# Projection products handed out six matmuls at a time in a fused four-stage kernel

## The chip, the cores and the metric

The kernel runs on one core of a Trainium2 chip. The metric is the device time of one execution in microseconds; lower is better. PE is the matrix engine (TensorE), DVE, ACT and POOL are the vector, scalar and GpSimd engines, SP is the queue that issues most transfers.

## The reference, cut to what matters

Two transformer blocks of width 1024 over a sequence of 512. In the first, a projection of the input feeds an RWKV-7 mixer (8 heads of 64) and a block-sparse attention (MoBA, 4 heads of 128), whose outputs together go through an output projection; then an MLP, a dilated attention of 8 heads with its own projections, and an MLP again. In the second block one projection feeds four mixers (S5, HGRN, FoX and mLSTM), followed by an output projection and a gated MLP. The RWKV mixer is the part that matters most below; each of its heads runs this recurrence over the 512 positions:

```python
def step(S, inp):
    r_t, w_t, k_t, v_t, a_t, b_t = inp
    sa = jnp.einsum('bhvk,bhk->bhv', S, a_t)
    S = S * w_t[:, :, None, :] + sa[..., None] * b_t[:, :, None, :] + v_t[..., None] * k_t[:, :, None, :]
    return S, jnp.einsum('bhvk,bhk->bhv', S, r_t)
...
_, y = lax.scan(step, jnp.zeros((B, H, N, N), f32), xs)
...
y = ((y - mu) * lax.rsqrt(var + RWKV_GN_EPS)).reshape(B, T, RWKV_DIM) * lnx_g + lnx_b
...
return y * g
```

The second block's mixers end in `mix = jnp.concatenate([y_a, y_b, y_c, y_d], axis=-1) @ w_out[l]`, where `y_d` is a headwise normalised mLSTM output times a sigmoid gate.

## The kernel before

**Stages.** By the trace's clock: RWKV and MoBA with their projection 0 to 388 us, MLP to 800, dilated attention with its projection to 1129, MLP to 1529, the four mixers of the second block with their projection ("block 2") to 1833, output projection and gated MLP to 2228. All data is fp32; every large product is made of three matmuls on values split into a high and a low part (`wh`/`wl` for weights, `acth`/`actl` for activations). ACT writes the high part (L228, L238), DVE the low part (L230, L239).

**Projections as filler.** `Kern.stream` (L254 to 283) is a Python generator. A task is one projection tile of 128 output columns over all 512 positions: eight row tiles k of the contraction, three matmuls of 128x512 each (L272, L273, L274, PSUM tile `gemm`). After every row tile it yields 0.64, its own estimate of the microseconds just issued. At k = 0 it also issues the previous task's evacuation and the next weights' transfer, at k = 6 the next weights' split. `Kern.early` (L285 to 303) does the same for the first half of the columns of the output projection, over the row tiles of the mixers' output that are already there (tile `pjps`, L356 to 358); it yields 0.64 after three matmuls too, and `Kern.project` does the second half of the columns afterwards.

**The planner.** `Kern.race` (L305 to 347) decides in which order code is emitted. Its chains are generators for the mixers; a chain yields the PE time and the latency of the step just issued. A chain is taken when its operands should be there by the planner's clock; otherwise, or when the debt `owed` is over 0.6, one turn of the filler is taken:

```python
if self.gemm is not None and (i is None or ready[i] > t or owed > 0.6):
    r = next(self.gemm, None)
    ...
    if r:
        t, owed, stuck = t + r, owed - r, 0
        owed = max(owed, 0)
...
    if r[0]:
        t = at + r[0]
        owed += keep * r[0]
```

`keep` is 0.65 in the RWKV stage and 0.5 in the dilated stage and block 2. When `stream` is at its end, `over()` puts `early` in its place, and what chains are left after both go out with no filler. A scheduler then simulates the program and sets the final order on each engine from this order. PE runs its instructions strictly in that order.

**The RWKV chain.** Four pairs of heads go one after another through `core` (L571 to 739): the inverse of a triangular matrix in five levels (L604 to 632: product `pinv` L610, mask `pm` on DVE L614, product `pinv` L624, addition `yc` on DVE L628; the last level has half the products), then `pg` (L647), `ptu` (L658), `pmc` (L675 to 677), `pqt` (L693), a chain of states with `pst` (L714) and `py` (L703, L704) beside it, and `py` again (L732). `tail` (L741 to 780) normalises: a sum (L749), a square, a second sum, an inverse root in small DVE steps, a product (L764), transposes `pyt` (L768), the gate `pgt` (L773, L775), the last product `ymix` (L778) and its split (L238, L239), from which the output projection's products read. Only the last pair has no later pair's work behind it.

**The end of block 2.** After the mLSTM's last products `mlo` (L1666) come DVE and ACT steps (L1668 to 1678), a head norm (L1523 to 1536, last step L1535), transposes `bkp` (L1543) for two row tiles of the mixers' output, gain and gate (L1686, L1688) and the split.

Of the kernel before, what the change touches and what calls it, by code (L numbers as in the profile page):

```python
# [105 lines left out]
class Kern:  # L106
# [147 lines left out]
    def stream(self, win, tasks, x, first=None, late=None):  # L254


        nc = self.nc
        xh, xl = x
        w = first or self.wload(win, tasks[0][0])
        for i, task in enumerate(tasks):  # L260
            m, evac = task[1:3]
            if len(task) > 3 and not task[3]():
                if late and i:
                    late[0](late[1])
                    late = None
                while not task[3]():
                    yield 0
            nxt = None
            ps = self.psG.tile([P, 512], F32, name="gemm", tag="g")
            n = len(w)  # L270
            for k, (h, l) in enumerate(w):
                nc.tensor.matmul(ps[0:m], lhsT=h[:, 0:m], rhs=xh[:, k, :], start=k == 0, stop=False)  # L272
                nc.tensor.matmul(ps[0:m], lhsT=h[:, 0:m], rhs=xl[:, k, :], start=False, stop=False)  # L273
                nc.tensor.matmul(ps[0:m], lhsT=l[:, 0:m], rhs=xh[:, k, :], start=False, stop=k == n - 1)  # L274
                if k == 0 and late:
                    late[0](late[1])
                if k == 0 and i + 1 < len(tasks):
                    nxt = self.wfetch(win, tasks[i + 1][0])
                if k == n - 2 and nxt:
                    w = self.wsplit(nxt)  # L280
                yield 0.64
            late = (evac, ps)
        late[0](late[1])

# [2099 lines left out]
```

## Time and profile before

| | us |
|---|---|
| median of three runs (lowest, highest) | 2234.99 (2234.35, 2239.33) |
| the profiled execution | 2230.15 |
| its span on the core | 2228.0 |
| PE busy in it | 2160.5 |
| DVE, ACT, POOL busy | 1265.1, 758.6, 382.0 |

The times from the rows below belong to the profiled execution; the comparison with another kernel goes by the medians, which here lie 5 us higher. A busy share says little by itself: matmuls that overlap count once in "busy", and a PE that is busy at a lower granted clock ("PEclk", 1.00 is 2.4 GHz, 0.50 is 1.2 GHz) gets less done.

### The profile page before, as it was taken

What the parts mean: (1) busy time and instruction counts of PE and PEld (TensorE: products, weight loads), DVE (VectorE), ACT (ScalarE), POOL (GpSimd) and SP (SyncE); (2) the same over time, 40 slices, a digit from 0 to 9 for tenths busy, and PEclk for the clock granted to TensorE, in tenths of its full rate; (3) what the DMA queues carried; (4) which work ended last, traced back from release to release, by engine and by line L of the source; (5) the groups of instructions that cost most, each with busy time, mean ns of one, the idle gap of its engine ahead of it and who ended that gap; (6) DMA issues with size and microseconds to landing.
All of it is one profiled execution on the core that took longest, in us unless ns stands there. A gap on an engine that the chain in (4) does not pass through costs nothing.

```text
span 2228.0 us, 37413 instructions
## 1 busy us (share of the span) xinstructions
PE 2160.5 (97%) x15646; PEld 1709.3 (77%) x15646; DVE 1265.1 (57%) x2528; ACT 758.6 (34%) x1218; POOL 382.0 (17%) x399
## 2 busy tenths in 40 slices
PE   8999999999999999999999999998999998999997
PEld 6666667888878877777788888877667778888886
DVE  6576666764444765656574444466755566344445
ACT  4332333423322433333342233235434354222221
POOL 0011111370056242332130000011320021000001
PEclk9999999999999999999999999998899999999999
DMA  4111114342333322222243233213211232233321
GB/s 142 49 40 40 49 40 170 97 131 95 100 100 113 126 77 67 67 68 66 86 139 94 90 104 95 93 45 132 63 45 46 92 104 95 95 97 98 99 76 38
DMA packets 56088, 192.80 MB, mean 87 GB/s; under 512 B 8208, under 2 KB 8720, under 8 KB 55408
## 3 DMA queue, kind: packets, MB, share of 16 engines
q1 hardware_dynamic: 52384, 184.11, 25.6%
q0 software_dynamic: 3536, 6.32, 0.9%
q8 instruction: 122, 2.00, 0.4%
q14 instruction: 46, 0.38, 0.1%
HBM read 181.98 MB, written 8.39 MB: 85 GB/s over the span
## 4 chain that ended last, share of the span: by engine, by line
PE 79%; DVE 10%; issue 4%; ACT 3%; DMA 2%; POOL 2%; SPq 0%; DVEq 0%; ACTq 0%; POOLq 0%
PE gemm L272 6%; PE mlpo L356 6%; PE mlpo L357 6%; PE mlpo L358 6%; PE gemm L273 5%; PE gemm L274 5%; PE mlps L249 4%; PE mlps L250 4%; PE mlps L251 4%; PE ffg L250 2%; PE ffg L251 2%; PE ffg L249 2%; PE ffu L250 2%; PE ffu L251 2%; PE ffu L249 2%
## 5 line engine op out<-in xcount | busy, mean ns | idle before, releaser
L228 ACT CAST wh<-wr 128x1024 fp32r<-128x1024 f32 (+1 forms) x311 | 323.4, 1044 | 762.3 <-PE mlpo L358 247.5
L230 DVE TENSOR_TENSOR wl<-wr,wh 128x1024 fp32r<-128x1024 f32 (+1 forms) x285 | 354.9, 1246 | 359.9 <-ACT wh L228 270.2
L272 PE MATMUL gemm<-acth,wh 128*128 128x512 f32 (+1 forms) x672 | 306.1, 456 | 7.8 <-ACT acth L238 6.4
L274 PE MATMUL gemm<-acth,wl 128*128 128x512 f32 (+1 forms) x672 | 271.8, 404 | 4.5 <-DVE wl L230 4.5
L273 PE MATMUL gemm<-actl,wh 128*128 128x512 f32 (+1 forms) x672 | 272.4, 405 | 0.0
L356 PE MATMUL mlpo<-wh,mlph 128*128 128x512 f32 x688 | 270.2, 393 | 0.3 <-DVE xres L1039 0.3
L357 PE MATMUL mlpo<-wl,mlph 128*128 128x512 f32 x688 | 269.6, 392 | 0.0
L358 PE MATMUL mlpo<-wh,mlpl 128*128 128x512 f32 x688 | 269.4, 392 | 0.0
L249 PE MATMUL mlps<-acth,wh 128*128 128x512 f32 x448 | 176.3, 394 | 0.0
L251 PE MATMUL mlps<-acth,wl 128*128 128x512 f32 x448 | 176.2, 393 | 0.0
L250 PE MATMUL mlps<-actl,wh 128*128 128x512 f32 x448 | 176.1, 393 | 0.0
L272 PEld LDWEIGHTS gemm<-acth,wh 128*128 128x128 f32 (+1 forms) x672 | 128.9, 192 | 59.1 <-issue 24.7
L274 PEld LDWEIGHTS gemm<-acth,wl 128*128 128x128 f32 (+1 forms) x672 | 128.9, 192 | 36.0 <-DVE wl L230 5.8
L356 PEld LDWEIGHTS mlpo<-wh,mlph 128*128 128x128 f32 x688 | 129.4, 188 | 29.3 <-DVE xres L1039 0.4
L358 PEld LDWEIGHTS mlpo<-wh,mlpl 128*128 128x128 f32 x688 | 129.1, 188 | 29.1 <-DVE mlpl L239 0.2
L357 PEld LDWEIGHTS mlpo<-wl,mlph 128*128 128x128 f32 x688 | 129.2, 188 | 28.6
L230 POOL TENSOR_TENSOR wl<-wr,wh 128x1024 fp32r<-128x1024 f32 (+1 forms) x26 | 71.2, 2763 | 446.0 <-ACT wh L228 424.1
L273 PEld LDWEIGHTS gemm<-actl,wh 128*128 128x128 f32 (+1 forms) x672 | 129.9, 193 | 22.9 <-issue 4.4
L1039 DVE SCALAR_TENSOR_TENSOR xres<-xres,mlpo 128x512 f32<-128x512 f32 x120 | 82.1, 685 | 105.3 <-PE mlpo L358 104.3
L251 PEld LDWEIGHTS mlps<-acth,wl 128*128 128x128 f32 x448 | 84.1, 188 | 19.7
L250 PEld LDWEIGHTS mlps<-actl,wh 128*128 128x128 f32 x448 | 84.2, 188 | 19.4
L249 PEld LDWEIGHTS mlps<-acth,wh 128*128 128x128 f32 x448 | 84.1, 188 | 19.5
(617 smaller groups left out, 3901.9 us busy)
## 6 DMA issues: line engine op xcount, KB each, us to landing
wr<-mlp_w SPq DMA_DIRECT2D x128, 512.0 KB, 3.6
wr<-ffn_w SPq DMA_DIRECT2D x66, 512.0 KB, 3.5
wr<-c_w_in SPq DMA_DIRECT2D x40, 512.0 KB, 3.6
wr<-ab_w_in SPq DMA_DIRECT2D x25, 512.0 KB, 3.6
wr<-w_in SPq DMA_DIRECT2D x24, 512.0 KB, 3.7
wr<-ab_w_out SPq DMA_DIRECT2D x8, 512.0 KB, 3.9
wr<-c_w_out SPq DMA_DIRECT2D x8, 512.0 KB, 3.7
wr<-w_out SPq DMA_DIRECT2D x8, 512.0 KB, 3.9
```

What stands on the lines that cost most here:

```text
L228: nc.scalar.copy(hi, raw)
L230: eng.tensor_tensor(lo, raw, hi.bitcast(F32), op=ALU.subtract)
L249: nc.tensor.matmul(ps, lhsT=hs, rhs=a, start=start and k == 0, stop=False)
L250: nc.tensor.matmul(ps, lhsT=hs, rhs=b, start=False, stop=False)
L251: nc.tensor.matmul(ps, lhsT=ls, rhs=a, start=False, stop=stop and k == n - 1)
L272: nc.tensor.matmul(ps[0:m], lhsT=h[:, 0:m], rhs=xh[:, k, :], start=k == 0, stop=False)
L273: nc.tensor.matmul(ps[0:m], lhsT=h[:, 0:m], rhs=xl[:, k, :], start=False, stop=False)
L274: nc.tensor.matmul(ps[0:m], lhsT=l[:, 0:m], rhs=xh[:, k, :], start=False, stop=k == n - 1)
L356: nc.tensor.matmul(ps, lhsT=a, rhs=h[:, c0 : c0 + n], start=start and k == 0, stop=False)
L357: nc.tensor.matmul(ps, lhsT=a, rhs=l[:, c0 : c0 + n], start=False, stop=False)
L358: nc.tensor.matmul(ps, lhsT=b, rhs=h[:, c0 : c0 + n], start=False, stop=stop and k == kt - 1)
L1039: self.K.nc.vector.scalar_tensor_tensor(xs, xs, f, ps, op0=ALU.mult, op1=ALU.add, accum_out=self.sums[:, t, c : c + 1])
```

## The change

In `stream` the generator gives back control after every second row tile instead of after every one, and reports twice the time. `early` still yields after three matmuls. Nothing else is edited; line numbers after this place are one higher.

```diff
@@ Kern.stream
                 if k == n - 2 and nxt:
                     w = self.wsplit(nxt)
-                yield 0.64
+                if k % 2:
+                    yield 1.28
             late = (evac, ps)
```

The instructions are the same in kind and number: 840 matmuls of filler in the RWKV stage (648 `gemm`, 192 output projection), 1056 in the dilated stage, 695 in block 2. Their order differs. In the RWKV stage they stood in 164 runs, of which 106 were runs of three and 17 of six; now in 101, of which 2 are of three and 77 of six. In the dilated stage there are 105 runs where there were 98, in block 2 86 where there were 110. At the point where the third pair's `pg` is issued, 468 `gemm` matmuls had gone out; now all 648 have, and 17 of the output projection.

PE in the state chain of the first pair, where `pst` is a step of the state and `py` the work beside it. Before:

```order
L714 MATMUL pst<-state,mt 64x64 x2
L272 MATMUL gemm<-acth,wh 128x512
L273 MATMUL gemm<-actl,wh 128x512
L274 MATMUL gemm<-acth,wl 128x512
L703 MATMUL py<-tu,arb 64x64
L704 MATMUL py<-v_tm,ark 64x64
L703 MATMUL py<-tu,arb 64x64
L704 MATMUL py<-v_tm,ark 64x64
```

The same place now:

```order
L715 MATMUL pst<-state,mt 64x64 x2
L272 MATMUL gemm<-acth,wh 128x512
L273 MATMUL gemm<-actl,wh 128x512
L274 MATMUL gemm<-acth,wl 128x512
L272 MATMUL gemm<-acth,wh 128x512
L273 MATMUL gemm<-actl,wh 128x512
L274 MATMUL gemm<-acth,wl 128x512
L704 MATMUL py<-tu,arb 64x64
L705 MATMUL py<-v_tm,ark 64x64
L704 MATMUL py<-tu,arb 64x64
```

Between two steps of the chain stand six filler matmuls in place of three.

PE in the inverse of the last pair (`a_3525`), two products of one level and the next level's first. Before:

```order
L610 MATMUL pinv<-yc,a_3525 32x32 x15
L272 MATMUL gemm<-acth,wh 128x512
L273 MATMUL gemm<-actl,wh 128x512
L274 MATMUL gemm<-acth,wl 128x512
L272 MATMUL gemm<-acth,wh 128x512
L273 MATMUL gemm<-actl,wh 128x512
L274 MATMUL gemm<-acth,wl 128x512
L624 MATMUL pinv_4087<-pm,xc 32x32 x32
L272 MATMUL gemm<-acth,wh 128x512
L273 MATMUL gemm<-actl,wh 128x512
L274 MATMUL gemm<-acth,wl 128x512
L897 MATMUL mopo<-mpt,mv 128x512
```

Now, the end of the last pair's inverse from the second product of level 4 on (`a_3798`, in the last level `a_3799`), with the products that follow it:

```order
L359 MATMUL pjps<-wh,actl 128x512
L625 MATMUL pinv_4208<-pm,xc 32x32 x32
L611 MATMUL pinv<-yc,a_3798 32x32 x32
L625 MATMUL pinv_4280<-pm,xc 32x32 x32
L611 MATMUL pinv<-yc,a_3798 32x32 x32
L625 MATMUL pinv_4352<-pm,xc 32x32 x32
L611 MATMUL pinv<-yc,a_3799 32x32 x16
L625 MATMUL pinv_4409<-pm,xc 32x32
L648 MATMUL pg_4432<-v_tm,aak 64x64 x5
L625 MATMUL pinv_4409<-pm,xc 32x32 x15
L648 MATMUL pg_4432<-v_tm,aak 64x64 x11
L659 MATMUL ptu<-rhs,ttc 64x128 x16
```

The first row is the last of 58 output-projection matmuls in one row. Behind it come 354 matmuls of the last pair's `core` and `tail` with no filler between them, up to the last `pgt`; the 108 output-projection matmuls that are left come after that, the first 12 of them on the last pair's row tile. Before, `gemm` runs stood between all levels, 26 output-projection matmuls lay between the steps of the last `core` and `tail`, and 166 came behind.

PE at the end of block 2, between the last `mlo` products and the transposes `bkp`. Before, the end of a row of 60 output-projection matmuls that follow `mlo`:

```order
L357 MATMUL pjps<-wl,acth 128x512
L358 MATMUL pjps<-wh,actl 128x512
L1543 MATMUL bkp<-consts,mo__16550 128x128 x4
L356 MATMUL pjps<-wh,acth 128x512
L357 MATMUL pjps<-wl,acth 128x512
L358 MATMUL pjps<-wh,actl 128x512
L356 MATMUL pjps<-wh,acth 128x512
L357 MATMUL pjps<-wl,acth 128x512
L358 MATMUL pjps<-wh,actl 128x512
L1543 MATMUL bkp<-consts,mo__16550 128x128 x4
```

Now, the end of a row of 15:

```order
L357 MATMUL pjps<-wh,acth 128x512
L358 MATMUL pjps<-wl,acth 128x512
L359 MATMUL pjps<-wh,actl 128x512
L1544 MATMUL bkp<-consts,mo__16607 128x128 x8
L357 MATMUL pjps<-wh,acth 128x512
L358 MATMUL pjps<-wl,acth 128x512
```

45 fewer matmuls stand between `mlo` and `bkp`, and none between the two sets of `bkp`. Earlier in block 2 there are now two rows of 158 and 126 mixer matmuls with no filler, each followed by a lump of 30 and 42 `gemm` matmuls.

## Rows read from the trace of the kernel before

**Rows 1.** The page's busy time by engine (share of the span) and count.
```profile
PE 2160.5 (97%) x15646; PEld 1709.3 (77%) x15646; DVE 1265.1 (57%) x2528; ACT 758.6 (34%) x1218; POOL 382.0 (17%) x399
```

**Rows 2.** The page's chain that ended last, shares of the span by engine.
```profile
PE 79%; DVE 10%; issue 4%; ACT 3%; DMA 2%; POOL 2%; SPq 0%; DVEq 0%; ACTq 0%; POOLq 0%
```

**Rows 3.** Windows: length, busy PE, PEld, DVE, ACT, POOL, clock, DMA share, GB/s.
```profile
0.00:388.00 388.00, 376.59 (x5513) 266.05 (x5514) 253.12 (x557) 134.03 (x242) 36.27 (x34) 1.00 0.23 76
...
800.00:1129.00 329.00, 316.02 (x1861) 246.01 (x1860) 200.72 (x449) 115.37 (x205) 97.16 (x62) 0.98 0.22 71
...
1529.00:1833.00 304.00, 290.19 (x2357) 216.44 (x2357) 191.18 (x432) 134.51 (x243) 53.95 (x73) 0.96 0.23 74
```

**Rows 4.** Timeline (start us, duration us, engine, line), PE in a state chain.
```profile
267.17 0.33 PE L714 MATMUL pst<-state,mt 64*64 64x64 f32 x4
267.43 0.51 PE L272 MATMUL gemm<-acth,wh 128*128 128x512 f32 x1
...
268.33 0.34 PE L703 MATMUL py<-tu,arb 64*64 64x64 f32 x4
...
268.99 0.50 PE L272 MATMUL gemm<-acth,wh 128*128 128x512 f32 x1
...
270.15 0.51 PE L272 MATMUL gemm<-acth,wh 128*128 128x512 f32 x1
...
270.96 0.39 PE L272 MATMUL gemm<-acth,wh 128*128 128x512 f32 x1
271.19 0.40 PE L273 MATMUL gemm<-actl,wh 128*128 128x512 f32 x1
...
271.75 0.33 PE L714 MATMUL pst<-state,mt 64*64 64x64 f32 x4
```

**Rows 5.** Timeline, one level of the inverse and the next level's first product.
```profile
145.13 0.75 PE L610 MATMUL pinv<-yc,a 32*32 32x32 f32 x64
...
147.01 0.39 DVE L614 TENSOR_TENSOR pm<-pinv,consts 128x256 f32<-128x256 f32 x1
...
147.61 0.75 PE L624 MATMUL pinv<-pm,xc 32*32 32x32 f32 x64
...
148.92 0.41 DVE L628 TENSOR_TENSOR yc<-pinv,yc 128x256 f32<-128x256 f32 x1
...
149.41 0.38 PE L610 MATMUL pinv<-yc,a 32*32 32x32 f32 x12
```

**Rows 6.** Timeline, the last pair from its first ptu product to its split.
```profile
326.00 1.09 PE L658 MATMUL ptu<-rhs,ttc 64*64 64x128 f32 x16
...
343.11 0.69 PE L732 MATMUL py<-state,qtb 64*64 64x64 f32 x18
...
345.35 0.69 DVE L749 TENSOR_REDUCE gs<-yk 128x8 f32<-128x512 f32 x1
...
355.24 0.62 ACT L238 CAST acth<-ymix 128x512 fp32r<-128x512 f32 x1
```

**Rows 7.** Windows as above: the last pair's end, then two stalls.
```profile
326.00:356.00 30.00, 29.48 (x342) 20.91 (x342) 21.97 (x70) 13.23 (x30) 1.20 (x2) 1.00 0.17 51
864.00:872.00 8.00, 6.41 (x25) 4.88 (x23) 3.77 (x6) 1.71 (x3) 2.12 (x2) 0.79 0.01 2
1605.00:1619.00 14.00, 12.28 (x105) 7.50 (x105) 10.05 (x27) 6.57 (x12) 2.84 (x4) 0.64 0.10 37
```

**Rows 8.** Timeline, in brackets the idle time before it and its releaser.
```profile
867.21 1.28 PE L1314 MATMUL dipo<-dpt,dv 128*128 128x128 f32 x6 [1.59 <-DVE dpt L1310]
```

**Rows 9.** Timeline, the end of block 2.
```profile
1789.33 2.45 PE L1666 MATMUL mlo<-mvv,mw 128*128 128x65 f32 x20
...
1801.80 1.23 DVE L1535 TENSOR_TENSOR mo__16550<-mo__16550,hnr 128x1024 f32<-128x1024 f32 x1
...
1805.30 0.60 PE L1543 MATMUL bkp<-consts,mo__16550 128*128 128x128 f32 x4
...
1807.38 0.62 ACT L238 CAST acth<-ymix 128x512 fp32r<-128x512 f32 x1 [0.76 <-DVE ymix L1688]
```

## The prediction

> **What bounds the kernel now.** I read the busy times first, then the chain of waits, then the stages one by one, and last the two places where the filler ends. PE is busy 2160.5 of 2228.0 us [rows 1], and 79% of the chain that ended last is PE's own work, against 10% on DVE [rows 2]. So the time is PE's work plus PE's idle time, and the change can act in three ways only: on what PE loses each time it goes from filler to a mixer's matmuls and back, on PE's idle time, and on its clock. Idle in the RWKV stage is 388.00 - 376.59 = 11.4 us, in the dilated stage 13.0, in block 2 13.8 [rows 3]. The two MLP stages and the last one have no such generator and are left out.
>
> The last pair of the RWKV stage deserves a look of its own. It has no later pair beside it, and yet PE is busy 29.48 of 30.00 us there, at a full granted clock [rows 7]. What keeps it busy is `gemm`, output-projection and MoBA work that the planner still had. The kernel before has its filler spread so that it lasts to the end.
>
> **Fewer switches: a gain.** A run of three filler matmuls takes from its start to the next chain matmul 268.33 - 267.43 = 0.90 us, a run of six 271.75 - 270.15 = 1.60 [rows 4]. Inside a run a matmul follows another after 271.19 - 270.96 = 0.23 us [rows 4], so three should take 0.69 and six 1.38. Both runs lose 0.21 or 0.22: the loss is one of the run's edges and does not grow with its length. On the other side of the edge, four `pst` matmuls take 267.43 - 267.17 = 0.26 us, while sixteen matmuls of a like size take 268.99 - 268.33 = 0.66, or 0.04 each [rows 4]; at that rate four are 0.17, and 0.09 is lost again. A run costs 0.2 to 0.3 us. I take 0.3, since both losses stand in the trace, and 0.2 as the other end.
>
> By the order, the RWKV stage has 164 - 101 = 63 runs fewer, block 2 has 110 - 86 = 24 fewer, the dilated stage 7 more: 80 runs fewer in all, at 0.3 a gain of **24 us** (16 at 0.2). This counts in full only where PE is the bound, which rows 1 and 3 bear out for nearly all of the stretch.
>
> The Trainium skill, TensorE: Matmul & The Clock Gate, section "Single matmul latency", gives an isolated matmul of 512 columns (398 + 512) / 2.4 = 379 ns and one in a stream about 216 ns, so by that page I estimate 0.16 us for a broken stream. The trace's spacing is 0.23 us in a run and its loss per run 0.2 to 0.3 [rows 4]; by the page's figure the gain would be 80 x 0.16 = 13 us and the time 11 us above my sum.
>
> **Where the filler runs out: the RWKV stage.** The planner's debt passes 0.6, a turn of 1.28 is taken, and the debt is cut to zero rather than carried below it. So twice the filler goes out for the same chain work, and it is used up early. The order shows it: all 648 `gemm` matmuls are out before the third pair's `pg`, where 468 were, and for the last pair 354 chain matmuls stand in a row with no filler. PE is in order; the 108 matmuls left lie behind and can't come forward. Here the chain's latency is bare.
>
> How long is the bare chain? One level of the inverse is two products of 0.75 us, DVE's 0.39 and 0.41, and handovers: 149.41 - 148.92 - 0.41 = 0.08 us from DVE to PE, 147.61 - 147.01 - 0.39 = 0.21 at the other product [rows 5]. That is 2.6 us with nothing in the way, and 149.41 - 145.13 = 4.28 as it stands with filler and other DVE work in the way [rows 5]; I take 3.0. From the second product of level 4 on there are half a level, two levels and a last one with half the products: 1.5 + 6.0 + 2.2 = 9.7 us. From `ptu` to the last `py` it takes 343.11 + 0.69 - 326.00 = 17.8 us with PE busy all the time [rows 6, 7]; without the foreign work, and with `pg` ahead of it, I take 16. The tail up to the split's first half takes 355.24 + 0.62 - 345.35 = 10.5 us [rows 6], some of it DVE work of MoBA; I take 10. Together about **36 us** (33 to 41). PE's own work in them: 4.5 in the levels (2 x 0.75 each, less in the halves) and, of the 29.48 us that PE is busy there [rows 7], about half by the listing of its matmuls, so some 18 us in all. Idle: 36 - 18 = **+18 us** (13 to 23). The next to be late behind it is the output projection's first twelve matmuls on the last row tile, and all that follow them.
>
> Ahead of that the planner also lacks filler for the end of the third pair. There MoBA heads still run and the fourth pair is beside it, so PE has other work: **+3** (0 to 8, the upper end a sixth of the 45 us of filler that went out earlier, 197 x 0.23).
>
> **The clock in that stretch.** Where PE stalls for 1.59 us [rows 8], the granted clock over the 8 us around it is 0.79; where it has little but a chain for 14 us, it is 0.64 [rows 7]. In the last pair's stretch it is 1.00 today [rows 7]. With half of it idle it will probably not stay so. At 0.64, 18 us of PE work become 18 / 0.64 = 28, and the restart of the output projection at a low clock adds about 2: +12 at most; at least 0. I take **+6**.
>
> **Block 2.** 24 runs fewer are in the sum above. Two rows of 158 and 126 mixer matmuls now have no filler: the nearest row, 14 us with a chain almost alone, has 14.00 - 12.28 = 1.7 us idle [rows 7]. Two of these at 2 us: **+4** (0 to 8). At the end, L1535 finishes 1801.80 + 1.23 - (1789.33 + 2.45) = 11.3 us after the last `mlo` [rows 9], hidden under 60 matmuls x 0.23 = 13.8 us. Without the weight split and other DVE work in it I take 9 us. Only 15 x 0.23 = 3.4 us of cover are left. From the first `bkp` to the end of the high half of the split are another 1807.38 + 0.62 - 1805.30 = 2.7 us [rows 9], covered today, then only by `bkp` itself (0.60). So 9 - 3.4 + 2.4 = **+8** (5 to 10). The clock there: **+2** (0 to 4).
>
> **Dilated stage.** Four heads have the stall of rows 8 now, because DVE's copy L1310 stands behind the next tile's softmax; in the new order four heads (others) have it again. No change beyond the runs.
>
> **The sum.** -24 + 18 + 3 + 6 + 4 + 8 + 2 = +17; less 0.5 for the idle that the last pair's stretch already has (30.00 - 29.48 [rows 7]). Against the profiled execution of 2230.15 us that is some 2246.5. The median of the three runs, 2234.99, lies 4.8 above the profiled one; the change is measured against that, so **2251 us**.
>
> **Rivals.**
> First, *not slower after all*: the bare stretches cost less than the switches save. For: if the inverse's levels come at 2.6 us, the tail at 9, and PE holds 2.4 GHz through stalls of under a microsecond each, the RWKV end costs 12 us, block 2's 7. Then -24 + 12 + 1 + 0 + 2 + 5 = -4, or 2231; with the block 2 rows at zero, 2228. Against: four of the six terms would have to fall to their lower ends together. It decides at 24 us: below this in both stages together the kernel is not slower. If a switch costs 0.5 us, not 0.3, it would come out the same way (-40), but no row shows more than 0.3.
>
> Second, *the low clock holds through both bare stretches and their restarts*: all the chain's own 18 us and the first 10 us of output projection behind it at 0.5 to 0.64, and the same at block 2's end with its 10 us restart. That is 18 + 4 for the first in place of 6, and 5 in place of 2: 2270. For it: 0.64 and 0.79 after far shorter gaps [rows 7, 8]. Against it: many short gaps are not one long one, and in the same stage PE keeps 1.00 now. The Trainium skill, TensorE: Matmul & The Clock Gate, section "Why this matters for your kernels", advises to leave no idle gaps between bursts of matmuls, or the clock drops; rows 7 and 8 agree with it as far as they go.
>
> Third, *the dilated stage moves*: the stalls disappear. One costs 1.59 us and (1 - 0.79) x 8 = 1.7 us of clock [rows 7, 8]; four are 13 us, so 2238. With stalls in all eight heads it would be 2264. Against both: the new order has as many heads with the copy behind the softmax.
>
> That the change does not do what it says is excluded by the order: 77 runs of six in the RWKV stage.
>
> **How the numbers follow.** The forecast has 0.50, the first rival 0.17, the second 0.18, the third 0.10 for no stalls and 0.05 for eight. The forecast's own range, its terms' bounds taken as independent, is about 2234 to 2268. The range over all cases leaves out the lower part of the first rival and the upper part of the second: **2229 to 2274**. About 0.2% (4.5 us) is what a measurement of this kernel can tell from no change, so faster means below 2230.5 and slower above 2239.5. Faster: most of the first rival, 0.13 with a little of the third. Same: the rest of these two and the forecast's lower end, 0.14. Slower: **0.73**.
>
> **What would show it.** Right: in the RWKV stage the filler's mean spacing falls, PE is busy only about half of some 36 us before the last `pgt`, with idle put down to DVE `pm`, `yc`, `yk`; the granted clock there is under 0.9; at block 2's end PE waits some 7 us for L1535. The stretch of RWKV before the last pair should be about 19 us shorter for the same matmuls. Wrong: if PE's busy share in the last pair's stretch stays above 0.8, or if the time before it shrinks by under 10 us, the terms were mis-sized; if the dilated stage differs by more than 5 us, the copies went otherwise than I read them.

## The result, and the profile after

The changed kernel takes 2274.18 us (2272.54 to 2276.09), the kernel before 2235.07 in the same comparison: ratio 1.0178, 95% interval 1.0165 to 1.0191. That is 39 us slower, where 16 were forecast, and 0.2 us beyond the stated range (2229 to 2274). The profiled execution of it took 2275.23 us with a span of 2273.1; against the profiled execution of before the difference is 45 us, since that one lies 5 us under its median.

The page of the kernel after, busy time by engine [against rows 1]:

```profile
PE 2182.2 (96%) x15646; PEld 1735.4 (76%) x15646; DVE 1272.9 (56%) x2528; ACT 758.1 (33%) x1218; POOL 396.9 (17%) x399
```

The instructions are the same in number, and yet PE is busy 21.7 us longer (2182.2 against 2160.5) besides being idle 23.4 us longer (90.9 against 67.5). The busy time is the part that I had forecast to fall.

The three mixer stages, cut at the first instruction of their neighbours (columns as in rows 3: length, busy PE, PEld, DVE, ACT, POOL, granted clock, DMA share, GB/s). Before:

```profile
0.00:396.10 396.10, 383.98 (x5552) 272.11 (x5552) 260.90 (x573) 139.89 (x251) 42.11 (x37) 1.00 0.23 76
793.60:1136.00 342.40, 329.18 (x1923) 256.64 (x1921) 212.55 (x472) 122.79 (x214) 106.18 (x67) 0.98 0.23 72
1512.50:1843.00 330.50, 313.85 (x2520) 238.28 (x2519) 204.86 (x466) 148.27 (x270) 61.20 (x76) 0.95 0.25 84
```

After:

```profile
0.00:420.60 420.60, 388.09 (x5552) 282.90 (x5552) 255.94 (x573) 140.30 (x251) 43.28 (x37) 0.95 0.22 72
818.00:1149.20 331.20, 322.98 (x1923) 252.38 (x1921) 224.54 (x472) 121.77 (x214) 118.67 (x67) 0.99 0.24 74
1525.70:1888.00 362.30, 336.98 (x2524) 256.78 (x2523) 206.43 (x467) 148.98 (x271) 62.29 (x76) 0.88 0.24 77
```

| stage | length | idle | PE busy | clock |
|---|---|---|---|---|
| RWKV | +24.5 | 12.1 to 32.5: +20.4 | +4.1 | 1.00 to 0.95 |
| dilated | -11.2 | 13.2 to 8.2: -5.0 | -6.2 | 0.98 to 0.99 |
| block 2 | +31.8 | 16.7 to 25.3: +8.7 | +23.1 | 0.95 to 0.88 |

These three make 45.1 us, the whole difference; the other stages take 1159.0 us in both. The clock has two levels, 2.4 and 1.2 GHz, so a mean of 0.95 over 420.6 us is 2 x 0.05 x 420.6 = 42 us at the lower one, where the same stage of before shows none. In block 2 it is 33 us before and 87 after.

The bare stretches, in the same columns: the last pair of the RWKV stage as a whole, two pieces of it, and three places in block 2 [against rows 7].

```profile
345.00:388.00 43.00, 28.47 (x713) 22.86 (x711) 18.32 (x53) 6.89 (x14) 1.61 (x3) 0.71 0.16 52
353.00:367.00 14.00, 11.26 (x246) 10.34 (x246) 3.16 (x8) 2.86 (x7) 0.40 (x1) 0.51 0.01 2
377.00:387.00 10.00, 4.54 (x8) 1.75 (x8) 4.91 (x19) 1.41 (x2) 1.21 (x2) 0.50 0.33 104
1617.00:1627.00 10.00, 3.45 (x10) 1.99 (x9) 9.29 (x25) 4.72 (x6) 1.85 (x3) 0.79 0.16 52
1637.00:1647.00 10.00, 9.99 (x112) 7.26 (x111) 0.77 (x2) 1.62 (x5) 0.00 (x0) 0.99 0.19 54
1647.00:1657.00 10.00, 10.00 (x154) 8.06 (x155) 1.59 (x3) 1.80 (x3) 0.00 (x0) 0.50 0.01 2
```

The first three show what was forecast: idle time, and a clock that drops with it; the fourth shows the same at a place that was not forecast. The last two show something else. From 1637 to 1657 PE is busy 19.99 of 20 us, and the clock falls all the same. The timeline there (start, duration):

```profile
1642.13 0.43 PE L1955 MATMUL s5y<-sF,sCA 128*32 128x63 f32 x16
1642.49 0.88 PE L1863 MATMUL hgo<-hiv,hfar 128*128 128x64 f32 x6
...
1645.36 0.25 PE L1833 MATMUL hgm<-hw 64*32 64x32 f32 x4
1645.55 0.32 PE L1837 MATMUL hgm<-hw 64*64 64x64 f32 x2
...
1647.18 0.65 PE L1955 MATMUL s5y<-sF,sCA 128*32 128x63 f32 x16
```

What PE does before the fall is narrow mixer matmuls, one after another, without a 128x512 product among them. The same sixteen matmuls take 0.43 us at 1642 and 0.65 at 1647. Twice more in this stage the clock falls inside a row of mixer matmuls with PE busy all the time:

```profile
1667.00:1677.00 10.00, 10.00 (x196) 7.90 (x198) 7.39 (x26) 3.25 (x6) 2.96 (x10) 0.85 0.18 54
1727.00:1737.00 10.00, 10.00 (x35) 7.55 (x34) 3.07 (x11) 2.86 (x8) 0.00 (x0) 0.58 0.01 2
```

The waits at the ends (in brackets the idle time before and its releaser), the RWKV tail first, then a stall in the middle of block 2 and block 2's end:

```profile
382.46 1.09 PE L769 MATMUL pyt<-consts,yk 128*128 128x128 f32 x4 [6.68 <-DVE yk L765]
388.68 0.80 PE L357 MATMUL pjps<-wh,acth 128*128 128x512 f32 x1 [1.43 <-ACT acth L238]
```

```profile
1624.39 2.07 PE L1950 MATMUL s5y<-su,sKT 128*128 128x512 f32 x2 [6.55 <-DVE sy L1960]
```

```profile
1849.35 1.97 PE L1544 MATMUL bkp<-consts,mo__16607 128*128 128x128 f32 x8 [5.78 <-DVE mo__16607 L1536]
```

These are the places that the prediction named, `yk` in the tail and the head norm before `bkp` [rows 6, 9], and one that it did not, at 1624.

### The profile page after: what moved, and what is told of

The parts are those of the page before. It is cut to its first block, busy times and chain, and to the rows that moved or that the text cites. A ratio compares the mean times of both kernels' runs of the same rounds, so it can differ in the third digit from the quotient of the medians.

```text
span 2273.1 us, 37407 instructions
## 1 busy us (share of the span) xinstructions
PE 2182.2 (96%) x15646; PEld 1735.4 (76%) x15646; DVE 1272.9 (56%) x2528; ACT 758.1 (33%) x1218; POOL 396.9 (17%) x399
## 4 chain that ended last, share of the span: by engine, by line
PE 44%; DVE 5%; issue 3%; ACT 2%; DMA 0%; POOL 0%; DVEq 0%; ACTq 0%; POOLq 0%
PE mlpo L358 3%; PE mlpo L357 3%; PE mlpo L359 3%; PE mlps L249 2%; PE mlps L250 2%; PE mlps L251 2%; PE gemm L272 2%; PE gemm L274 2%; PE gemm L273 2%; PE ffg L250 2%; PE ffg L251 2%; PE ffg L249 2%; PE ffu L250 2%; PE ffu L251 2%; PE ffu L249 2%
## 5 line engine op out<-in xcount | busy, mean ns | idle before, releaser
L272 PE MATMUL gemm<-acth,wh 128*128 128x512 f32 (+1 forms) x672 | 296.9, 442 | 8.1 <-ACT acth L238 7.5
L358 PEld LDWEIGHTS mlpo<-wl,mlph 128*128 128x128 f32 x688 | 129.2, 188 | 28.6
```

The lines of the kernel that those rows point to most:

```text
L358: nc.tensor.matmul(ps, lhsT=a, rhs=l[:, c0 : c0 + n], start=False, stop=False)
```

## The experiments

**One stage at a time.** A flag on `stream` switches the pairs on for one stage; the other stages keep the order of before.

```diff
-                yield 0.64
+                if not pair:
+                    yield 0.64
+                elif k % 2:
+                    yield 1.28
```

> Two row tiles a turn in the RWKV stage alone. If the stages act on their own, this costs what the RWKV stage of the changed kernel lost by its trace, 24.5 us (420.6 against 396.1 at the first MLP product): about 2259. By the prediction's own terms (-19 for switches, +18, +3, +6) it would be +8, 2243. If something acts across stages, it is neither.

Measured: 2260.75 against 2232.19, ratio 1.0126 (1.0111 to 1.0141), +28.6 us.

> Two row tiles a turn in the dilated stage alone. By the trace of the changed kernel this stage is 11.1 us shorter (331.2 against 342.3): about 2224. The prediction held it at +2: 2237. If its gain only follows from what the stage before left behind, no change: 2235.

Measured: 2220.61, ratio 0.9943 (0.9924 to 0.9962), -11.6 us.

> Two row tiles a turn in block 2 alone. By the trace of the changed kernel the stage is 30.3 us longer (360.7 against 330.4): about 2265. By the prediction's terms (-7 for switches, +4, +8, +2) it would be +7: 2242. Clock theory: stretches of mixer matmuls without filler at a granted clock of 0.5 though PE is not idle, near 90 us of low clock in the stage.

Measured: 2253.34, ratio 1.0094 (1.0079 to 1.0109), +21.1 us.

The three make 38 us, as the whole change does (39): in sum the stages act on their own. One by one they agree less well. The RWKV stage costs 4 us more than in the trace of the whole change, and block 2 costs 21 alone and had cost 32 there, though its order is the same (the 30.3 of the expectation is 31.8 by the rows above). The row of 158 mixer matmuls without filler, in the whole change and in block 2 alone (the profile counts each of these matmuls twice):

```profile
1635.50:1658.10 22.60, 22.53 (x318) 17.24 (x317) 4.61 (x9) 4.11 (x9) 0.00 (x0) 0.73 0.09 25
```

```profile
1618.20:1635.80 17.60, 17.46 (x318) 13.26 (x317) 4.36 (x8) 4.39 (x9) 0.00 (x0) 1.00 0.10 32
```

The same matmuls, next to no idle time in either, and 5.0 us between them: the clock fell in this row once and stayed at 1.00 once. The stage as a whole varies too, without any change of its order. Block 2 of the kernel with pairs in block 2 alone, then with pairs in the RWKV stage alone, and, in a second answer, with pairs in the dilated stage alone:

```profile
1513.30:1866.70 353.40, 324.94 (x2520) 248.62 (x2520) 205.84 (x466) 148.90 (x271) 61.56 (x76) 0.91 0.24 79
```

```profile
1537.00:1876.10 339.10, 321.04 (x2524) 243.48 (x2524) 207.12 (x468) 148.77 (x271) 61.28 (x76) 0.93 0.25 82
```

```profile
1501.70:1826.40 324.70, 308.63 (x2521) 234.03 (x2521) 205.91 (x466) 148.53 (x271) 61.14 (x76) 0.97 0.26 86
```

The last two run block 2 in the order of before, and so does the kernel before (330.50 us at 0.95). One order, three executions: 324.7, 330.5 and 339.1 us at clocks of 0.97, 0.95 and 0.93, with idle of 16.1, 16.7 and 18.1. The low-clock time by these means is 19, 33 and 47 us; PE is busy 12.4 us longer for 28 us more at 1.2 GHz, 0.44 us each. That is the price of the low clock with the order unchanged. By the same view block 2 of the whole change has 87 us of it and the same stage alone 64 (2 x 0.09 x 353.4). What made the clock fall longer in one execution than in another of the same order, no run here shows.

**Useless work in the bare rows.** Where the planner wants filler and there is none, matmuls of full width that change nothing are issued. In block 2 they go into a PSUM tile that is never read; in the RWKV stage a zero operand is added into the waiting sums of the output projection.

```diff
+                if self.junk is not None and i is not None:
+                    ps = self.psG.tile([P, 512], F32, name="junk", tag="g")
+                    for k in range(3):
+                        self.nc.tensor.matmul(ps, lhsT=self.junk[:, k, 0:P], rhs=self.junk[:, k, :], start=k == 0, stop=k == 2)
+                    t, owed = t + 0.64, max(owed - 0.64, 0)
+                    continue
```

> As the run with pairs in block 2 alone, but where the planner wants filler and the projection cannot give any, three matmuls of 128x512 on the activations go out into a PSUM tile that nobody reads: 132 matmuls, 45 runs, 132 x 0.23 = 30 us of useless PE work, of which the stage's added idle (8 us) takes up a part. Latency theory (the loss is bare waits, the clock a small part): the useless work costs its 30 us less 8, so some 20 us slower than with pairs in block 2 alone. Clock theory (the loss is the 1.2 GHz clock in stretches without filler): granted clock 1.00 in these stretches, low-clock time down by some 45 us, which gives back over 20 us: within 8 us of the run without the useless work, or faster.

Measured: 2260.93, ratio 1.013 (1.0113 to 1.0147), 7.6 us above the run with pairs in block 2 alone. Its block 2:

```profile
1513.20:1873.40 360.20, 342.54 (x2656) 260.06 (x2656) 205.40 (x466) 148.08 (x269) 61.11 (x76) 0.98 0.23 77
```

Against 353.40 us at 0.91: the trace has 135 useless matmuls (the expectation counted 132), 31 us of work, the stage is 6.8 us longer, idle fell from 28.5 to 17.7. So 31 - 10.8 - 6.8, some 13 us, came back from the clock, more if the added runs have a price. The 7.6 us lie just inside the clock theory's 8 and far from the 20 of the latency theory.

```diff
+                if self.zt is not None and self.sent and i is not None and owed > 0.6:
+                    for k in range(3):
+                        self.nc.tensor.matmul(self.po[k], lhsT=self.zt, rhs=self.zx[k], start=False, stop=False)
+                    t, owed = t + 0.64, max(owed - 0.64, 0)
+                    continue
```

> As the run with pairs in the RWKV stage alone, but when the output projection has to wait for the last row tile, 128x512 matmuls with a zero operand are added into its PSUM tiles (the sums stay the same): by the order 57 of them in a row before the last pair's bare rows, and 69 in 19 places between the bare products. Useless work: 57 x 0.23 = 13 us added outright, 69 x 0.23 + 18 x 0.2 = 20 us between, of which the 13 us of idle that the bare stretch has can take up that much. Latency theory: 13 + 20 - 13 = 20 us slower than without them, stage 442 us (422.7), 2281. Clock theory: the granted clock stays at 1.00 from the 57 on, the 34 us of low clock there disappear and give back 12 to 17 us: stage 425 to 430, 2264 to 2269.

Measured: 2274.6 against 2234.67, ratio 1.0187 (1.0164 to 1.021). The RWKV stage, with pairs in the RWKV stage alone and then with the zero products:

```profile
0.00:422.70 422.70, 390.68 (x5552) 284.58 (x5552) 255.91 (x573) 140.06 (x251) 43.23 (x37) 0.94 0.22 71
```

```profile
0.00:435.90 435.90, 412.87 (x5679) 299.18 (x5679) 256.44 (x574) 140.65 (x252) 43.29 (x37) 0.98 0.21 69
352.00:404.00 52.00, 46.65 (x799) 33.55 (x797) 17.37 (x52) 5.91 (x14) 1.61 (x3) 0.97 0.07 22
```

By the means 51 us of low clock became 17. The clock in the last pair's stretch is 0.97, where the same stretch had 0.71 under the whole change, and the stage is 13.2 us longer. That lies between the two expectations (425 to 430 by the clock theory, 442 by the latency theory). 126 x 0.23 = 29 us of work were added and 9.0 us of idle were filled, so about 7 us came back, or some 10 with 0.16 us (see below) for each of the 18 added runs. The clock's part in the RWKV loss is there, but smaller than half of the low-clock time. A chain that waits for DVE as well as for PE would explain it; no run here shows that this is the reason.

**Spending without lumps.** Next the kernel before, with the planner's `keep` doubled (0.65, 0.5, 0.5 become 1.3, 1.0, 1.0): one row tile a turn, asked for twice as often.

> The kernel before with the planner's keep doubled in all three mixer stages (1.3, 1.0, 1.0): turns of one row tile, but twice the filler for the same chain work. By the order, bare rows of 130, 107, 272 and 226 chain matmuls at the end of the RWKV stage and of 136 and 143 in block 2; the dilated stage as before. If spending the filler early is what costs, this is slower than before by 25 to 55 us without any run of six being asked for: 2260 to 2290, with idle and low clock at the same places. If it is the length of a turn that costs (chain steps behind six matmuls), it is within 10 us of before.

Measured: 2279.48, ratio 1.0211 (1.0191 to 1.023), +46 us. Its RWKV stage and block 2:

```profile
0.00:413.20 413.20, 383.76 (x5553) 279.75 (x5553) 257.43 (x573) 140.37 (x251) 45.25 (x37) 0.97 0.22 73
1530.50:1891.20 360.70, 333.15 (x2524) 254.36 (x2524) 205.61 (x467) 148.89 (x271) 60.98 (x76) 0.89 0.23 77
```

The same picture as under the change (29.4 and 27.6 us idle, clocks of 0.97 and 0.89), with no turn of six matmuls asked for: filler that is spent early is missing later. This run alone does not clear the length of a run, since turns taken one behind the other still make 38 runs of six in its RWKV stage (17 before, 77 under the change, counted in the traces). The debt rule below does: 44 runs of six, none of the filler spent earlier, and no such loss. The converse, the changed kernel with `keep` halved (0.325, 0.25, 0.25):

> The changed kernel with the planner's keep halved in all three mixer stages (0.325, 0.25, 0.25): turns of two row tiles, asked for half as often by debt. By the order the bare rows shrink to 141 and 171 in the RWKV stage (133, 237, 354 under the change) and 103 in block 2 (158, 126); runs in the RWKV stage 115. If early spending and the clock behind it are the loss, it goes down with the bare rows: idle in the RWKV stage 20 to 25 us (32.5), low clock there under 25 us (41), time between 2235 and 2258. If six matmuls at a time are the loss, it stays at 2270 or more.

Measured: 2250.66 against 2233.93, ratio 1.0074 (1.0054 to 1.0095), +17 us: less than half of the loss is left. Idle in its RWKV stage is 26.5 us (expected 20 to 25) and some 33 us there are at the low clock (expected under 25), so a little more stays than I had expected. By stage it is not even: the dilated stage keeps its gain, block 2 takes 345.1 us, 14.6 above before where the whole change has 31.8, but the RWKV stage takes 417.2 us, and there 21.1 of the 24.5 us are left. In its trace 564 `gemm` matmuls are out at the third pair's `pg` (468 before, 665 filler matmuls under the change), and the wait for `yk` in the last tail is 7.03 us long (6.68 under the change). A turn of two row tiles taken for a wait, and not for debt, may be what still overspends; no run parts the two.

**Fewer switches without early spending.** Two turns of one row tile in a row, only where the debt has grown to 1.24:

```diff
-            if self.gemm is not None and (i is None or ready[i] > t or owed > 0.6):
+            if self.gemm is not None and (i is None or ready[i] > t or owed > lim):
...
-                    t, owed, stuck = t + r, owed - r, 0
+                    t, owed, stuck, lim = t + r, owed - r, 0, 0.6
...
+                lim = 1.24
```

> Two turns of one row tile in a row, but only where the planner's debt has reached 1.24, so that no more filler goes out than before. By the order 125 runs in the RWKV stage (164), 103 in block 2 (108), the dilated stage as before; no bare row over 100 matmuls anywhere. If the switches cost 0.2 to 0.3 us each and early spending is the fault of the change, 44 runs fewer gain 9 to 13 us: ratio 0.994 to 0.996. If fewer switches bring nothing, the ratio is 1.00.

Measured: 2236.49, ratio 1.0015 (1.0006 to 1.0024). No gain. The RWKV stage cut at the last pair's `pg`, before and then with these pairs:

```profile
0.00:321.20 321.20, 310.34 (x4976) 215.76 (x4976) 209.34 (x442) 108.19 (x197) 29.32 (x30) 1.00 0.19 61
321.20:396.10 74.90, 73.64 (x578) 56.35 (x577) 51.55 (x131) 31.69 (x54) 12.80 (x7) 1.00 0.41 141
```

```profile
0.00:316.40 316.40, 303.37 (x4971) 215.07 (x4971) 206.92 (x442) 108.31 (x197) 28.59 (x29) 1.00 0.19 60
316.40:401.40 85.00, 79.01 (x585) 59.91 (x584) 52.08 (x132) 31.51 (x54) 16.48 (x9) 0.96 0.37 130
```

Up to the last pair PE is busy 7.0 us less at a full clock, but 6 filler matmuls fewer (1.4 us) stand in that stretch too. Up to the third pair's `pg` both traces hold the same 468 filler matmuls, in 106 runs before and in 80 with these pairs:

```profile
0.00:229.80 229.80, 221.35 (x3625) 154.01 (x3625) 149.36 (x314) 80.95 (x145) 16.99 (x20) 1.00 0.21 68
```

```profile
0.00:227.30 227.30, 217.16 (x3620) 153.76 (x3620) 146.26 (x305) 79.55 (x140) 17.93 (x20) 1.00 0.22 69
```

PE is busy 4.2 us less for 26 runs fewer: 0.16 us a run. Up to the last pair idle took back 2.2 us. Then the last pair's stretch is 10.1 us longer, again by a wait in the tail and the clock behind it. (In the order of before this stage took 400.5 us in one other run, that with the copy on ACT, and 396.1 to 396.5 in the rest; so the 401.4 here say little without the ratio.)

```profile
355.23 1.09 PE L769 MATMUL pyt<-consts,yk 128*128 128x128 f32 x4 [4.46 <-DVE yk L765]
355.96 0.78 PE L357 MATMUL pjps<-wh,acth 128*128 128x512 f32 x1
```

**The dilated stage.** The copy L1310 taken from DVE, so that it can't stand behind a softmax:

```diff
-            h0 = (t + 1) // 2 * P
+            h0 = 0
```

> The kernel before with the copy L1310 of the dilated stage left to ACT alone, so that it can't stand behind DVE's softmax. If the stage's gain under the change is the four stalls of 1.6 us and the clock that falls behind them, it appears here without any pairs: idle down by some 5 us, low clock from 13.7 us to about 3, some 10 us faster (ratio 0.995). If it comes from the runs of six, nothing here: 1.00.

Measured: 2218.48, ratio 0.994 (0.9925 to 0.9956), -14.7 us, with the generator as before. Its dilated stage:

```profile
798.00:1129.30 331.30, 323.71 (x1923) 254.24 (x1921) 207.04 (x448) 125.74 (x214) 105.77 (x67) 0.98 0.24 74
```

331.3 us, as under the change (331.2). What PE waited for before the products L1314, in us and times, before, after and with the copy on ACT:

```profile
  DVE dpt L1310: 6.5, 4
```

```profile
  DVE dpt L1311: 4.2, 4
```

```profile
  ACT dpt L1311: 1.4, 3
```

The low clock did not go as expected (0.98, 13 us by the mean, where 3 were expected): in this run it fell at the stage's start (808 us) and near its end (1102 us), and nowhere behind these stalls. The idle did, 7.6 us against 13.2.

> The copy L1310 on ACT alone and two row tiles a turn in the dilated stage alone. If both act by the same four stalls and the clock behind them, the second adds nothing: ratio 0.994 as the copy alone. If runs of six gain by themselves, another 3 to 10 us: 0.990 to 0.993.

Measured: 2217.32, ratio 0.9932 (0.9906 to 0.9958), its dilated stage 324.7 us at 0.99. The trace says that pairs add something to the copy, 6.6 us; the times cannot tell it (0.9932 and 0.9940, the intervals overlap). The copy alone shows what the stalls are worth, about the whole gain of the stage. It does not show that pairs gain by nothing else: PE's first long wait in the stage, for POOL before `disc`, is 3.11 us before and 3.13 with the copy, and 1.97 under the change and 1.96 with both. So pairs shorten a wait that the copy leaves as it is.

**Combinations.**

> Pairs of turns by debt in all stages, as in the run above, and the generator's two row tiles a turn in the dilated stage alone. If the two gains add: 10 + 11 us, ratio about 0.990 (2213 against 2235).

Measured: 2225.82, ratio 0.9974 (0.9958 to 0.999): less than the dilated pairs alone, as the debt rule costs here too (its RWKV stage takes 405.6 us in the trace).

> The copy L1310 on ACT alone, and two turns in a row where the debt reaches 1.24, save while the last entry of a stage's first chain runs (in the RWKV stage the last pair), where the old rule holds. By the order 133 runs in the RWKV stage (164). 31 runs at 0.15 to 0.25 us are 5 to 8 us less there if the last pair keeps its cover; with the copy's 13 to 15 us, ratio 0.990 to 0.992. If the stage's end loses again what the switches gain, 0.994.

Measured: 2223.28 against 2233.93, ratio 0.9945 (0.9926 to 0.9964): the copy's gain and nothing of the switches'. Its RWKV stage is 396.9 us long, PE busy 381.75 of it: 2.2 us less than before and idle 3.0 more. Five kernels are faster than before, by 0.3 to 0.7%. The four that lead (pairs in the dilated stage, the copy on ACT, both, and the copy with the debt rule, ratios 0.9932 to 0.9945) can't be told apart by their times.

## Why the prediction was right or wrong

**Early spending: right, in mechanism and in idle time.** The sum had +18 and +3 for the RWKV stage, less 0.5; its idle grew by 20.4. For block 2 it had +4 and +8; idle grew by 8.7 in the whole change and by 28.5 - 16.7 = 11.8 in the stage alone. At its end PE waits 5.78 and 1.30 us for the norm and the split, 7.1 where the sum had 8 (in which 2.4 stands for 2.7 - 0.60 = 2.1). The +4 is right by luck: the row of 158 idles 0.1 us and that of 126 about 1, and the wait of 6.55 us at 1624 was in no term. The run with `keep` doubled spends early in turns of one row tile and loses 46 us; the debt rule makes runs of six without early spending and stays within 0.2% of before.

**The clock: the step that failed.** I gave it +6 in the RWKV stage, +2 at the end of block 2 and nothing in block 2's middle. With 0.16 us a run, the busy time of RWKV should have fallen by 63 x 0.16 = 10; it rose by 4.1, so the clock took some 14 (by the zero products it is nearer 12: 42 us of low clock at 10/34 of a us each). In block 2 the busy time should have fallen by 4 and rose by 23.1: 27, and 15 in the stage alone (at 0.44 us for each us of low clock, 24 and 14). The mistake was to look for the clock only where PE would idle. For the two rows of 158 and 126 mixer matmuls I priced the idle time, read from the 14 us at 1605 [rows 7], and left their clock at nothing, although that row itself showed 0.64. Nor was that row like them: its low clock stands behind a wait for DVE, and filler runs in it at the lower clock (0.50 from 1609 to 1619).

```profile
1608.01 0.48 PE L1852 MATMUL hgf<-hw 64*128 64x128 f32 x2 [1.72 <-DVE hiv L1478]
...
1608.85 0.80 PE L272 MATMUL gemm<-acth,wh 128*128 128x512 f32 x1
1609.45 0.63 PE L273 MATMUL gemm<-actl,wh 128*128 128x512 f32 x1
```

Under the change the row of 158 had no such wait, and a clock of 0.73. What the filler did for the clock was not in the sum: with 135 wide matmuls put back into the bare rows of block 2 its mean clock rose from 0.91 to 0.98. Why the same row ran at 1.00 in the run with pairs in block 2 alone stays open.

**Fewer switches: right in sign, too large.** 0.3 us a run was read from three neighbouring gaps [rows 4]; 0.16 is what the debt rule's 26 runs fewer show over 227 us. The term is -13, not -24. The Trainium skill, TensorE: Matmul & The Clock Gate, sections "Single matmul latency" and "Back-to-back issue gap", had led to an estimate of 0.16, which the prediction set beside its sum; the run agrees with that and not with my 0.3. The 0.09 that I read on the chain's side of the edge [rows 4] set four `pst` matmuls against the rate of sixteen `py` matmuls; the debt rule's run shows nothing of it.

**The dilated stage: wrong.** I counted heads with the copy behind the softmax, found four before and four after, and forecast no change; it gave 11.2 us. The order says which instruction comes first, not how long PE waits. On DVE, before, three steps of the next tile's softmax stand ahead of the copy:

```profile
863.45 1.56 DVE L1295 TENSOR_TENSOR ds<-ds 128x128 f32<-128x128 f32 x1
864.93 1.30 DVE L1294 TENSOR_SCALAR dcl<-consts,dstat 128x4 f32<-128x4 f32 x1
866.27 0.69 DVE L1297 TENSOR_TENSOR de<-ds,dcl 128x512 f32<-128x512 f32 x1
866.88 0.28 DVE L1310 COPY dpt<-dipt 128x128 f32<-128x128 f32 x1
```

Under the change it is one of these steps and a product of the rotary embedding (`rope`):

```profile
889.45 0.66 DVE L1298 TENSOR_TENSOR de<-ds,dcl 128x512 f32<-128x512 f32 x1
890.04 1.75 DVE L1245 TENSOR_TENSOR dz<-dz,rope 32x512 f32<-32x512 f32 x1
891.72 0.27 DVE L1311 COPY dpt<-dipt 128x128 f32<-128x128 f32 x1
```

The stalls are shorter, 4.2 us in four where there were 6.5, and the clock did not fall behind them [against rows 7, 8]:

```profile
892.05 1.17 PE L1315 MATMUL dipo<-dpt,dv 128*128 128x128 f32 x6 [1.23 <-DVE dpt L1311]
```

```profile
889.00:897.00 8.00, 6.77 (x32) 5.16 (x31) 4.86 (x7) 2.41 (x4) 4.33 (x2) 1.00 0.19 66
```

1.23 us and a clock of 1.00, where it had been 1.59 and 0.79. This comes near the third rival's price (13), which was given a tenth, but not quite by its mechanism: the stalls did not disappear, and the shorter wait before `disc` is part of the gain.

**The rivals.** The first is gone: the bare stretches cost more than the switches save. The second, the low clock held through the bare stretches at 2270, came nearest to the time, partly by luck: it had 22 us for the clock in the RWKV stage, where 12 to 14 are shown, it kept the switches at 24, and it put the clock's loss at the ends of the stages and missed the middle of block 2. The rule of the Trainium skill that stood beside it (TensorE: Matmul & The Clock Gate, section "Why this matters for your kernels"), to leave no idle gaps between bursts, fits the RWKV tail, with its wait of 6.68 us and a clock of 0.50; the stretch at 1637 us, without a gap, goes beyond it.

**The sum once more**, on the profiled executions: -13 for the switches, +24 of idle (20.4 + 8.7 - 5.0), and for the clock 14 + 27 less some 7 in the dilated stage, 34: +45, where 45.1 were measured. That it comes out is bookkeeping, as these clock terms are what is left of the busy time. With the prices from other runs, 12 for the RWKV stage, 54 x 0.44 = 24 for block 2 and -3 for the dilated stage, it is +44.

## What to carry to other kernels

Filler that covers another engine's waits is a stock: a coarser turn does not only come in larger pieces, it is spent sooner unless the accounts carry what was overspent, and the end of the stage, where there is nothing else to run, pays for it. In block 2 wide matmuls in the bare rows also brought the clock back up (0.91 to 0.98), so read the granted clock beside the busy time, and let the range of a forecast hold a stretch without filler at 1.2 GHz, even when the order shows PE with enough to do. And before a stall is declared unchanged because the order at it looks alike, ask which instructions now stand ahead of it and how long they take.

## What the runs showed of the hardware that was not expected

The granted clock fell from 1.00 to 0.50 at 1647 us with PE busy 9.99 of the 10 us before, on matmuls of 32 to 384 columns only; the same row of matmuls ran at 1.00 from end to end in another program. One order of block 2, run in three programs, had mean clocks of 0.97, 0.95 and 0.93 and lengths of 324.7, 330.5 and 339.1 us. Nor did the clock go the same way behind the same stalls. In the kernel before, three of the four stalls of 1.58 to 1.66 us in the dilated stage were followed by a clock of 0.66 over the next 5 us and one by 1.00; with pairs in the RWKV stage alone, where the dilated stage has the order of before, it was one of four (1.57 to 1.62 us) and three.
